# A hybrid layer on one core: DeltaNet outputs formed by channel, with the decay carried by the queries and one norm factor per token

## The chip, the cores and the metric

The kernel runs on one core of one Trainium2 chip. The time is device microseconds (us) of one execution. Each run of the program gives one time, and the median of several runs stands for the kernel. One execution was also recorded by the hardware profiler; rows of that record are called the trace.

The core has five engines that run their own instruction streams side by side: TensorE (PE in the rows; PEld is its weight load), VectorE (DVE), ScalarE (ACT), GpSimd (POOL) and SyncE (SP), which here issues nearly all DMA transfers, one after the other, in its own order. An instruction waits, with all behind it on its engine, until the tiles it reads are written and the buffers it writes are free.

## The reference

The layer takes x of 1024 tokens by 1024 channels (float32). After an RMSNorm one projection feeds two mixers. Mixer A is a gated DeltaNet of 4 heads with 128 channels each; mixer B is a dilated attention of 8 heads. Their outputs are joined and projected, added to x, and followed by a gated MLP and a last RMSNorm. The change lies in mixer A:

```python
qa = l2norm(silu(causal_dwconv(q))) * 128 ** -0.5    # also ka (without the factor) and va
gam = exp(cumsum(g))                                  # decay within a chunk
q_dec = gam * qa
attn  = dec_incl * (q k^T) * beta
# chunk after chunk, S the state (key channels by value channels):
u = u_v - w_k S
o = q_dec S + attn u                                  # tokens by channels
S = g_end * S + k_end^T u
o_a = rmsnorm(o, gdn_norm_w) * silu(z)                # per token and head, over 128 channels
```

`l2norm(x)` is x * rsqrt(sum(x^2) + eps), and `rmsnorm` is x * rsqrt(mean(x^2) + eps) * w, with eps = 1e-6.

## The kernel before

Activations lie with channels on the 128 partitions and the 1024 tokens along the free axis. A dense product of the input projection takes one column of 128 output channels: 48 matmuls of 128x512, since each fp32 product is made of three products of split halves (`xhi`, `xlo`, `whi`, `wlo`) over 8 slices of x and two halves of the tokens. There are 25 such columns, in the order of the table `DENSE` (line 42): keys, queries and values of the heads, the attention's columns, and last the four z columns, the gates.

The order of TensorE's instructions is fixed when the program is built. `Weave` (lines 49 to 120) runs generators as streams with a level each; it models TensorE's time and the time at which each tile will be ready, and always takes the ready stream of the lowest level. So the DeltaNet's chains (level 1), the preparation of keys, queries and values (3 and 4), the attention (5) and the output projection (8) are strewn among the dense matmuls (9), which fill what is left. `yield wv.need(...)` puts a stream to sleep until a tile is ready by the model, `wv.until(name)` until another stream has set a name. All matmuls carry `TOKEN` and keep this order on the chip; the order of the other engines follows from a scheduler. Buffers are rotating slots under a tag ("qa" has 4, "kT*" 4 in two parts, "kt" 4, "go" 2).

Per head of mixer A the steps are as follows. `kprep`, `qprep` and `vprep` take the convolved keys, queries and values. `qprep` (from line 641 on) transposes the queries in eight blocks of 128 tokens and sums their squares per token (`tokens`, line 568), makes the factor `rq` on VectorE and GpSimd (a power of -1/2), forms the masked products `at` of queries and keys, and stores `at` and the plain queries in DRAM (`atpark`, `qpark`). A block inverse per chunk follows, `forward_sub` with later merges, whose 32x32 blocks pass through DRAM (`xdram`, `xtdram`). When all heads are ready, `chain(h)` (line 809) goes through the 8 chunks. Each chunk makes the output twice: from the state (not for the first chunk) and from `at`, both as tokens by channels, in two halves of a PSUM bank:

```python
if c:
    mm(po[:, P:2 * P], qT, st, 0.215)
mm(po[:, :P], at, w, 0.215)
```

ScalarE scales the one by `rq`, VectorE adds the other times `gq` (`rq` times the decay), and ScalarE sums the squares of the result per token. After the last chunk, GpSimd makes `ms` to its power -1/2 and multiplies the whole output by it, and `finish(h)` transposes it back to channels by tokens (eight transposes), scales by the norm's weight `gw2` and stores it in `mixer`. When a z column is done, `dense` reloads the head's output as `og` and `gate` multiplies it with silu(z).

Of the kernel before, what the change touches and what calls it, by code (L numbers as in the profile page):

```python
# [144 lines left out]
def hybrid_layer(tc, I, out):  # L145
# [99 lines left out]
    mixer = dp.tile([8, P, S], F32, name="mixer")  # L245
    mdram = dp.tile([H, 32, 1024], F32, name="mdram")
    gdram = dp.tile([NCH * H, P], F32, name="gdram")
    xdram = dp.tile([H, 32, 1024], F32, name="xdram")
    xtdram = dp.tile([H, 32, 1024], F32, name="xtdram")
    apark = dp.tile([4, 2, P, S], F32, name="apark")  # L250
# [19 lines left out]
    def v8(t):  # L270
        return t.rearrange("p (c t) -> p c t", c=NCH)
# [69 lines left out]
    ve.memset(ones, 1.0)  # L341
    tri = tile_(sp, [P, P], F32, "tri", "r0", 1)
    sy.dma_start(tri, I["tri"])
    pick = const("pick", [P, 32])
    ve.memset(pick, 0.0)
    ve.memset(pick[:, 8:9], 1.0)
    gcw = const("gcw", [P, 12, 4], I["gcw"])
    gnw = const("gnw", [P, 1], I["gnw"])
    alog = const("alog", [P, H], bass.AP(tensor=I["a_log"].tensor, offset=I["a_log"].offset, ap=[[0, P], [1, H]]))
# [61 lines left out]
    def gates():  # L411

        yield from wv.until("rst")
        ba = sp.tile([P, NCH, 8], F32, name="ba")
        ve.tensor_tensor(ba, bat[:, :, :8], rst[:, :, None].to_broadcast([P, NCH, 8]), op=OP.mult)
        ac.activation(beta, ba[:, :, :H], AF.Exp, scale=-1.0)
        ve.tensor_scalar(beta, beta, 1.0, None, op0=OP.add)
        ve.reciprocal(beta, beta)
        zt = sp.tile([P, NCH, H], F32, name="zt")
        ve.tensor_tensor(zt, ba[:, :, H:], dtb[:, None, :].to_broadcast([P, NCH, H]), op=OP.add)  # L420
        az = sp.tile([P, NCH, H], F32, name="az")
        ac.activation(az, zt, AF.Abs)
# [12 lines left out]
        grow = tile_(sp, [NCH * H, P], F32, "grow", "osq", 1)  # L435
        ac.activation(grow, pt[:NCH * H, P:2 * P], AF.Copy)
        sy.dma_start(gdram, grow)
        ve.tensor_copy(gc, pt[:, :NCH * H].rearrange("p (c h) -> p c h", c=NCH))
# [45 lines left out]
    def gate(og, xr, anchor=None):  # L484
        y = A("zz", "ev")
        insts = [ac.activation(y, xr, AF.Tanh, scale=0.5),
                 ve.scalar_tensor_tensor(y, y, 1.0, xr, op0=OP.add, op1=OP.mult),
                 ve.tensor_tensor(og, og, y, op=OP.mult)]
        last["og"] = insts[2:]
        if anchor is not None:  # L490
            after(insts[0], anchor[0], "the softmax goes first")
            after(insts[1], anchor[1], "the softmax goes first")
# [4 lines left out]
    G = [dict() for _ in range(H)]  # L497
    T = {}
    gated = {}

    def first_keys():
        xr = [scaled(pst[2 * h:2 * h + 2], "xr", tag=("ev", "ev", "qa")[h]) for h in range(3)]
# [5 lines left out]
    def dense():  # L508
# [8 lines left out]
        for i, col in enumerate(DENSE):  # L517
# [22 lines left out]
            if kind == "k":  # L540
                T["k", h] = conv_silu(xr, 4 + h, "kT", "kT*")
                wv.add(3, kprep(h))
            elif kind == "q":
                q = conv_silu(xr, h, "qT", "qa")
                wv.add(4, qprep(h, q))
            elif kind == "v":
                v = conv_silu(xr, 8 + h, "vT", "qa")
                wv.add(4, vprep(h, v))
            elif kind == "z":
                og = gated[h] = A("og", "kT*")  # L550
                sy.dma_start(og, mixer[h])
                if i + 1 < len(DENSE):
                    put_off.append((og, xr))
                else:
                    gate(og, xr)
            else:
                if col[2] < 2:
                    sy.dma_start(apark[h, col[2]], xr)
                else:
                    t = A("avt", "ev")  # L560
                    ve.transpose(t.rearrange("p (c n j) -> p n c j", c=4, n=NCH), by_block(xr))
                    for b in range(4):
                        sq_.dma_start(avdram[h].rearrange("u x (b j) -> b u x j", b=4)[b],
                                     t[32 * b:32 * b + 32].rearrange("u (x j) -> u x j", j=32))
                wv.done.add(col)
        wv.done.add("dense")

    def tokens(src, dst, scale=None, ss=None):
# [15 lines left out]
                    ua.activation(sq, pt[:, c * P:(c + 1) * P], AF.Square, accum_out=ss[:, i:i + 1])  # L584
        return dst

    def kprep(h):
        d = G[h]
        kT = T["k", h]
# [3 lines left out]
        dec = A("dec", ("dv", "dw")[h % 2])  # L593
        gend = small("gend")
        gel = small("gel")
        rows = gdram.rearrange("(c h) t -> h c t", h=H)[h]
        sy.dma_start(v8(dec), bass.AP(tensor=rows.tensor, offset=rows.offset, ap=[[0, P]] + list(rows.ap)))
# [43 lines left out]
    def qprep(h, qT):  # L641
        d = G[h]
        yield from wv.until(("k", h))
        yield wv.need(qT, slack=SLACK)
        ssq = small("ssq")
        yield from tokens(qT, None, None, ssq)
        ve.tensor_scalar(ssq, ssq, 128.0, 128.0 * EPS, op0=OP.mult, op1=OP.add)
        rq = small("rq", 4)
        rsqrt(rq, ssq, NCH)
        at = A("at", "qa", shape=(P, NCH, P))  # L650
        for c0 in range(0, NCH, 4):
            pt = yield from next_bank("atr")
            for c in range(4):
                cs = slice((c0 + c) * P, (c0 + c + 1) * P)
                mm(pt[:, c * P:(c + 1) * P], d["kT"][:, cs], qT[:, cs], 0.215)
            for c in range(4):
                i = c0 + c
                ve.scalar_tensor_tensor(at[:, i, :], pt[:, c * P:(c + 1) * P], d["bp"][:, i:i + 1],
                                               d["dec"][:, i * P:(i + 1) * P], op0=OP.mult, op1=OP.mult)
        sy.dma_start(atpark[h], at.rearrange("p c t -> p (c t)"))  # L660
        gq = small("gq", 4)
        ve.scalar_tensor_tensor(gq, ngam[:, :, h], -1.0, rq, op0=OP.mult, op1=OP.mult)
        sy.dma_start(qpark[h], qT)
        d.update(rq=rq, gq=gq)
        wv.done.add(("q", h))

    def vprep(h, vT):
# [143 lines left out]
    def chain(h):  # L811
# [2 lines left out]
            yield from wv.until(("m", i))  # L814
            yield from wv.until(("v", i))
        d = G[h]
        kT, ktok, vtok, yt, ge, rq, gq, ke = [d[n] for n in ("kT", "ktok", "vtok", "yt", "ge", "rq", "gq", "ke")]
# [5 lines left out]
        ms = small("ms", 4)  # L823
        tg = str(h)
        st = None
        for c in range(NCH):
# [31 lines left out]
                    uv.scalar_tensor_tensor(sn, st, ge[:, c:c + 1], ps[:, 2 * P:3 * P], op0=OP.mult, op1=OP.add)  # L858
            yield wv.need(w, qa, slack=HOP)
            po = yield from next_bank("atr")  # L860
            if c:
                mm(po[:, P:2 * P], qT, st, 0.215)
            mm(po[:, :P], at, w, 0.215)

            ua.activation(vtok[:, cs], po[:, :P], AF.Copy, scale=rq[:, c:c + 1])
            if c:
                uv.scalar_tensor_tensor(vtok[:, cs], po[:, P:2 * P], gq[:, c:c + 1], vtok[:, cs], op0=OP.mult,
                                        op1=OP.add)
            if c < NCH - 1:
                st = sn  # L870
            osq = tile_(sp, [P, P], F32, "osq", "osq", 1)
            ua.activation(osq, vtok[:, cs], AF.Square, accum_out=ms[:, c:c + 1])
            wv.done.add(("c", h, c))

        uv.tensor_scalar(ms, ms, 1.0 / 128, EPS, op0=OP.mult, op1=OP.add)
        rsqrt(ms, ms, NCH)
        po_.tensor_tensor(v8(vtok), v8(vtok), ms[:, :, None].to_broadcast([P, NCH, P]), op=OP.mult)
        wv.add(1, finish(h, vtok))

    def finish(h, osb):  # L880
        for hh in range(2):
            pt = yield from next_bank("atr", osb, slack=0.8)
            for c in range(4):
                i = 4 * hh + c
                tp(pt[:, c * P:(c + 1) * P], osb[:, i * P:(i + 1) * P])
            ot = tile_(sp, [P, 512], F32, "ot", "t2", 2)
            ac.activation(ot, pt, AF.Copy, scale=gw2)
            sy.dma_start(mixer[h][:, half(hh)], ot)
        wv.done.add(("o", h))

    def by_block(t):
        return t.rearrange("p (n c u) -> p n c u", n=NCH, c=4)
# [817 lines left out]
    wv.add(9, dense())  # L1713
    for h in range(H):
        wv.add(1, chain(h))
    wv.add(5, attention())
    wv.add(8, out_proj())
    wv.add(0, mixer_splits())
# [64 lines left out]
```

## Time and profile before

| | |
|---|---|
| median of 3 runs | 1191.49 us (1191.37 to 1192.41) |
| the profiled execution | 1191.63 us |
| its span in the trace | 1189.8 us |
| granted TensorE clock | 0.998 |
| TensorE busy | 1180.1 us, 6994 matmul records |
| VectorE busy | 965.4 us |
| ScalarE busy | 573.2 us |
| GpSimd busy | 54.6 us |
| DMA moved | 156.91 MB |

The profiled execution's time holds 1.83 us outside the span. In the groups, a row names line, engine, operation, the tile written and the tiles read, the shape and the number of instructions, then the busy time in us, the mean length of one in ns, and the engine's idle time ahead of them with what ended it. In a timeline a row begins with the start and the length in us; x8 joins eight instructions that follow each other, and square brackets hold the idle time ahead. TensorE overlaps its matmuls, so the lengths of neighbours add up to more than the time that passes; starts tell what one costs. Lines 139 and 141 are those of the helpers that record every operation of the other engines, and 192 and 196 those of all matmuls and transposes, so the tiles' names tell the steps apart.

### The profile page before, as it was taken

To read this page: it belongs to the slowest core of one execution; us is meant where nothing else is said; L and a number is where in the kernel's file an instruction comes from. 1 tells how busy PE (TensorE), PEld (TensorE's weight loads), DVE (VectorE), ACT (ScalarE), POOL (GpSimd) and SP (SyncE) were. 2 spreads that over 40 slices of the span, in tenths; PEclk is the share of its full clock that TensorE was granted. 3 is DMA by queue.
4 is the path that set the end of the run, shared out by engine and by line. 5 is a ranking of instruction groups with operands and counts; after the bars stand their busy time and mean duration, and the time that the engine had idled before them with its cause. 6 is when DMAs were issued, how large, how long until landed. Compare 5 with 4: busy or idle time off the path is not lost.

```text
span 1189.8 us, 18253 instructions
## 1 busy us (share of the span) xinstructions
PE 1180.1 (99%) x6994; PEld 975.9 (82%) x6994; DVE 965.4 (81%) x1545; ACT 573.2 (48%) x1122; POOL 54.6 (5%) x49
## 2 busy tenths in 40 slices
PE   9999999999999999999999999999999999999997
PEld 7888888888777777888888888888888888888887
DVE  7776996474677787677998898989889889898987
ACT  7473444363434444555554444545444553546452
POOL 0212001013000000000000000000000000000001
PEclk9999999999999999999999999999999999999999
DMA  7423457647552414343221313122231395356734
GB/s 239 107 94 84 114 144 163 201 149 186 166 147 72 99 37 151 142 159 107 89 92 68 107 53 107 57 103 81 80 102 58 120 377 202 124 178 220 239 98 160
DMA packets 114520, 156.91 MB, mean 132 GB/s; under 512 B 54368, under 2 KB 65408, under 8 KB 114432
## 3 DMA queue, kind: packets, MB, share of 16 engines
q1 hardware_dynamic: 113712, 155.21, 41.4%
q8 instruction: 55, 0.90, 0.3%
q10 hardware_dynamic: 720, 0.53, 0.1%
q14 instruction: 33, 0.27, 0.1%
HBM read 117.68 MB, written 38.03 MB: 131 GB/s over the span
## 4 chain that ended last, share of the span: by engine, by line
PE 97%; DVE 1%; ACT 0%; issue 0%; DVEq 0%; ACTq 0%
PE ps L192 47%; PE pa L192 20%; PE dw L192 18%; PE pc L192 10%; PE ps L201 1%; PE ps L196 1%; PE warm L192 0%; DVE x1h L139 0%; ACT sm L141 0%; DVE sm L141 0%; PE pd L192 0%; DVE avt L139 0%; DVE aqkv L139 0%; DVE wke L141 0%; DVE ct L141 0%
## 5 line engine op out<-in xcount | busy, mean ns | idle before, releaser
L192 PE MATMUL dw<-pr 128*128 128x512 f32 (+1 forms) x984 | 211.4, 376 | 0.0
L192 PEld LDWEIGHTS dw<-pr 128*128 128x128 f32 x984 | 176.7, 188 | 33.7
L192 PE MATMUL ps<-xhi,whi 128*128 128x512 f32 x448 | 183.7, 410 | 0.0
L192 PE MATMUL ps<-xhi,wlo 128*128 128x512 f32 x448 | 175.2, 391 | 0.0
L192 PE MATMUL ps<-xlo,whi 128*128 128x512 f32 x448 | 174.9, 391 | 0.0
L192 PE MATMUL pa<-T,pair 128*128 128x512 f32 x528 | 126.8, 389 | 0.0
L192 PEld LDWEIGHTS pa<-T,pair 128*128 128x128 f32 x528 | 99.1, 188 | 20.6
L192 PEld LDWEIGHTS ps<-xhi,whi 128*128 128x128 f32 x448 | 84.2, 188 | 18.9 <-issue 2.7
L192 PEld LDWEIGHTS ps<-xhi,wlo 128*128 128x128 f32 x448 | 84.1, 188 | 18.3
L192 PEld LDWEIGHTS ps<-xlo,whi 128*128 128x128 f32 x448 | 84.4, 188 | 14.9 <-DVE xlo L139 0.3
L139 ACT ACTIVATE u<-pa 128x512 f32<-128x512 f32 x44 | 26.4, 599 | 114.4 <-PE pa L192 114.4
L139 DVE SCALAR_TENSOR_TENSOR y<-xu,fcw,y 128x1023 f32<-128x1023 f32 (+1 forms) x44 | 56.4, 1281 | 22.1 <-ACT y L139 22.0
L139 ACT ACTIVATE pr<-wd 128x1024 fp32r<-128x1024 f32 x33 | 35.0, 1061 | 73.4 <-DVE wd L139 35.8
L192 PE MATMUL pa<-B,A 128*128 128x512 f32 x264 | 63.5, 389 | 0.0
L192 PE MATMUL pc<-B,pair 128*128 128x512 f32 x264 | 63.4, 389 | 0.0
L192 PE MATMUL pc<-T,S 128*128 128x512 f32 x264 | 63.4, 389 | 0.0
L192 PE MATMUL pa<-T,S 128*128 128x512 f32 x264 | 63.4, 389 | 0.0
L139 DVE TENSOR_TENSOR wst<-wst 128x512 f32<-128x512 f32 x88 | 60.4, 686 | 0.8
L139 ACT ACTIVATE whi<-wst 128x1024 fp32r<-128x1024 f32 (+2 forms) x38 | 38.5, 1013 | 46.5 <-PE ps L192 38.9
L192 PE MATMUL ps<-B,pair 128*128 128x512 f32 x252 | 60.5, 389 | 0.0
L141 ACT ACTIVATE sm<-sm,mx 128x128 f32<-128x128 f32 (+7 forms) x64 | 35.5, 556 | 49.7 <-DVE mx L141 49.7
L192 PEld LDWEIGHTS pa<-T,S 128*128 128x128 f32 x264 | 49.6, 188 | 10.3
(248 smaller groups left out, 2229.8 us busy)
## 6 DMA issues: line engine op xcount, KB each, us to landing
wst<-in_wu SPq DMA_DIRECT2D x44, 512.0 KB, 3.7
wd<-in_wd SPq DMA_DIRECT2D x44, 512.0 KB, 4.4
wst<-in_wi SPq DMA_DIRECT2D x25, 512.0 KB, 4.2
upark<-y SPq DMA_DIRECT2D x22, 512.0 KB, 3.6
r<-upark SPq DMA_DIRECT2D x22, 512.0 KB, 9.9
wa<-in_wd SPq DMA_DIRECT2D x22, 256.0 KB, 3.0
apark<-aqkv SPq DMA_DIRECT2D x8, 512.0 KB, 2.7
wst<-in_wo SPq DMA_DIRECT2D x8, 512.0 KB, 3.6
```

Of the source, the lines that this page charges most:

```text
L139: return getattr(eng, op)(*a, **kw)
L141: return getattr(eng, op)(*a, **kw)
L192: tc.stamp_issue_order_token(nc.tensor.matmul(dst, lhs, rhs, start=start, stop=stop, **kw).ins, TOKEN)
L196: tc.stamp_issue_order_token(nc.tensor.transpose(dst, src, ident).ins, TOKEN)
L201: tc.stamp_issue_order_token(nc.tensor.transpose(dst, src[rows], ident[rows, rows]).ins, TOKEN)
```

## The change

Outputs of the chain are formed as channels by tokens. The matmuls' operands change places and both products add up in one PSUM region. For that the queries carry their decay: `gates` stores exp(gc) as rows in DRAM (`gamdram`), `qprep` loads a head's row to all partitions (`qd`), GpSimd multiplies it by the queries, and `qd` is stored as `qpark`. The queries are no longer transposed. Their squares, scaled by 128 x eps, are stored in `qsqpark`.

The two norms (of the query and of the output) become one factor per token, the power -1/2 of a single sum: over the 128 channels, (sum of o^2 + the scaled sum of q^2) / 128, plus a constant (`eps2`). `finish` runs once for all heads: per head it reloads the queries' squares, ScalarE squares the output, GpSimd adds both (`osq`); then 16 matmuls with a selecting matrix (`picked(h)`) sum over channels, into rows of one bank; ScalarE copies the sums out, four DMAs store them (`sdram`), one DMA reloads them as 128 rows of 32 (`ft`), GpSimd takes the power, and they are stored (`fdram`). At each z column the head's factors are loaded to all partitions (`fB`) and GpSimd multiplies `og` by them. `gate` now brings in the norm's weight `gw2`.

```diff
@@ qprep(h, qT)
-        ssq = small("ssq")
-        yield from tokens(qT, None, None, ssq)
-        ve.tensor_scalar(ssq, ssq, 128.0, 128.0 * EPS, op0=OP.mult, op1=OP.add)
-        rq = small("rq", 4)
-        rsqrt(rq, ssq, NCH)
+        qd = A("qd", "qa")
+        to_all(v8(qd), gamdram.rearrange("(c h) t -> h c t", h=H)[h])
...
         sy.dma_start(atpark[h], at.rearrange("p c t -> p (c t)"))
-        gq = small("gq", 4)
-        ve.scalar_tensor_tensor(gq, ngam[:, :, h], -1.0, rq, op0=OP.mult, op1=OP.mult)
-        sy.dma_start(qpark[h], qT)
-        d.update(rq=rq, gq=gq)
+        po_.tensor_tensor(qd, qd, qT, op=OP.mult)
+        sy.dma_start(qpark[h], qd)
+        ac.activation(qT, qT, AF.Square, scale=128.0 * EPS ** 0.5)
+        sy.dma_start(qsqpark[h], qT)
@@ chain(h)
+            po = po[:, :P]
             if c:
-                mm(po[:, P:2 * P], qT, st, 0.215)
-            mm(po[:, :P], at, w, 0.215)
-
-            ua.activation(vtok[:, cs], po[:, :P], AF.Copy, scale=rq[:, c:c + 1])
-            if c:
-                uv.scalar_tensor_tensor(vtok[:, cs], po[:, P:2 * P], gq[:, c:c + 1], vtok[:, cs], op0=OP.mult,
-                                        op1=OP.add)
+                mm(po, st, qT, 0.215, True, False)
+            mm(po, w, at, 0.215, c == 0, True)
+            ua.activation(vtok[:, cs], po, AF.Copy)
             if c < NCH - 1:
                 st = sn
-            osq = tile_(sp, [P, P], F32, "osq", "osq", 1)
-            ua.activation(osq, vtok[:, cs], AF.Square, accum_out=ms[:, c:c + 1])
             wv.done.add(("c", h, c))
-
-        uv.tensor_scalar(ms, ms, 1.0 / 128, EPS, op0=OP.mult, op1=OP.add)
-        rsqrt(ms, ms, NCH)
-        po_.tensor_tensor(v8(vtok), v8(vtok), ms[:, :, None].to_broadcast([P, NCH, P]), op=OP.mult)
-        wv.add(1, finish(h, vtok))
+        sy.dma_start(mixer[h], vtok)
+        wv.done.add(("e", h))
@@ finish: once for all heads (before: per head, 8 transposes, 2 scaled copies, 2 stores)
+    def finish():
+        for h in range(H):
+            yield from wv.until(("e", h))
+            osq, qsq = A("osq", "kT*"), A("qsq", "kt")
+            osqs.append(osq)
+            sy.dma_start(qsq, qsqpark[h])
+            ac.activation(osq, G[h]["vtok"], AF.Square)
+            po_.tensor_tensor(osq, osq, qsq, op=OP.add)
+        for h in range(H):
+            wv.done.add(("o", h))
+        pt = yield from next_bank("atr", *osqs, slack=1.0)
+        for h in range(H):
+            for g in range(4):
+                o = 32 * g
+                mm(pt[o:o + 32, :256], picked(h), by_quarter(osqs[h])[:, g], 0.107, h == 0, h == H - 1,
+                   tile_position=(0, o))
+        sums = tile_(sp, [P, 256], F32, "sums", "t2", 2)
+        ac.activation(sums, pt[:, :256], AF.Identity, scale=1.0 / 128, bias=eps2)
+        for g in range(4):
+            sq_.dma_start(sdram.rearrange("h (c g i) -> g h c i", g=4, i=32)[g],
+                          sums[32 * g:32 * g + H].rearrange("h (c i) -> h c i", i=32))
+        ft = tile_(sp, [P, 32], F32, "ft", "osq", 1)
+        flat = "h (a t) -> (h a) t"
+        sq_.dma_start(ft, sdram.rearrange(flat, t=32))
+        f4 = ft.rearrange("p (a t) -> p a t", t=NCH)
+        po_.tensor_tensor(f4, f4, mhalf[:, None, :].to_broadcast([P, 4, NCH]), op=OP.pow)
+        sq_.dma_start(fdram.rearrange(flat, t=32), ft)
+        wv.done.add("f")
@@ dense(), z columns, and gate()
+                yield from wv.until("f")
                 og = gated[h] = A("og", "kT*")
                 sy.dma_start(og, mixer[h])
+                if not fB:
+                    fB.append(A("fB", "go"))
+                to_all(fB[0], fdram[h])
+                po_.tensor_tensor(og, og, fB[0], op=OP.mult)
...
-                 ve.tensor_tensor(og, og, y, op=OP.mult)]
+                 ve.scalar_tensor_tensor(og, og, gw2, y, op0=OP.mult, op1=OP.mult)]
```

`to_all(dst, rows)` is a DMA that reads the same rows for each of the 128 partitions.

On TensorE, at the end of a head's chain, before (vtok is the head's output, xhi, xlo, whi and wlo the dense matmuls, ct the state, qat the loaded queries and `at`):

```order
L192 MATMUL ps<-r,um 128x128
L192 MATMUL ps<-ct,kT 128x128
L196 MATMUL ps<-ident,vtok 128x128 x4
L192 MATMUL ps<-xhi,whi 128x512
L192 MATMUL ps<-xlo,whi 128x512
L192 MATMUL ps<-xhi,wlo 128x512
L192 MATMUL ps<-wke,ktok 128x128
L192 MATMUL ps<-ct,qat 128x128
L192 MATMUL ps<-w,qat 128x128
```

And after, at the same place:

```order
L192 MATMUL ps<-wke,ktok 128x128
L192 MATMUL ps<-qat,ct 128x128
L192 MATMUL ps<-qat,w 128x128
L192 MATMUL ps<-xhi,whi 128x512
L192 MATMUL ps<-xlo,whi 128x512
L192 MATMUL ps<-xhi,wlo 128x512
L192 MATMUL ps<-ct,kT 128x128
```

The four transposes of vtok are gone, and the two output matmuls of a chunk stand where they stood, with their operands changed.

On GpSimd, from the queries to the block inverse, a piece of the difference (rq is the power for the queries, xi and x the buffers of the inverse, nk the keys' factor):

```order
 L139 TENSOR_TENSOR nk<-ssk,phalf 128x8 x4
+L139 TENSOR_TENSOR qd<-qd,qT 128x1024
 L139 MEMSET xi 128x1024
 L139 AFFINE_SELECT xi<-xi 128x1024
-L139 TENSOR_TENSOR rq<-ssq,mhalf 128x8 x3
-L139 MEMSET x_1709 128x1024
-L139 MEMSET x_1723 128x1024
-L139 TENSOR_TENSOR rq<-ssq,mhalf 128x8
-L139 COPY mark<-x_1723 1x1
+L139 TENSOR_TENSOR qd<-qd,qT 128x1024 x2
+L139 MEMSET x_1663 128x1024
+L139 MEMSET x_1677 128x1024
```

Two multiplications by the decay come between the inverse's first steps and its later ones, in the place of the powers. Further on, before the attention's gates, GpSimd's order after is this (pb is a tile of the attention's probabilities):

```order
L139 TENSOR_TENSOR osq<-osq,qsq 128x1024
L139 TENSOR_TENSOR ft<-ft,mhalf 128x32
L139 TENSOR_TENSOR og<-og,fB 128x1024
L139 MEMSET pb 128x512
L139 TENSOR_TENSOR og<-og,fB 128x1024 x3
L139 MEMSET pb 64x256
L139 MEMSET pb 128x512 x2
```

The multiplications by the factor stand between the memsets of the attention.

On SP, after the norm factor's sums, after the change (avt and in_wi are the attention's values and the next weights):

```order
L139 DMA og<-mixer 128x1024
L139 DMA sdram<-sums 32x1x32 x4
L139 DMA ft<-sdram 128x32
L139 DMA fdram<-ft 128x32
L139 DMA fB<-fdram 128x1024
L139 DMA mixer<-oT 128x512
L139 DMA fB<-fdram 128x1024
L139 DMA wst<-in_wi 128x1024
```

The factor's way through DRAM stands ahead of a weight load, and SP issues nothing else until each step's data are there.

More of the change, by code (lines that the diff above doesn't have):

```diff
@@ L247, in hybrid_layer @@
     gdram = dp.tile([NCH * H, P], F32, name="gdram")
+    gamdram = dp.tile([NCH * H, P], F32, name="gamdram")
+    qsqpark = dp.tile([H, P, S], F32, name="qsqpark")
+    sdram = dp.tile([H, S], F32, name="sdram")
+    fdram = dp.tile([H, S], F32, name="fdram")
     xdram = dp.tile([H, 32, 1024], F32, name="xdram")
@@ L343, in hybrid_layer, with picked @@
     sy.dma_start(tri, I["tri"])
-    pick = const("pick", [P, 32])
-    ve.memset(pick, 0.0)
-    ve.memset(pick[:, 8:9], 1.0)
+    picks = const("picks", [P, 64])
+    ve.memset(picks, 0.0)
+    ve.memset(picks[:, 32:33], 1.0)
+    eps2 = const("eps2", [P, 1])
+    ve.memset(eps2, 128.0 * EPS * EPS)
+    def picked(j):
+        return picks[:, 32 - j:64 - j]
+    pick = picked(8)
     gcw = const("gcw", [P, 12, 4], I["gcw"])
@@ L437, in gates @@
         sy.dma_start(gdram, grow)
+        gamrow = tile_(sp, [NCH * H, P], F32, "gamrow", "w0", 1)
+        ac.activation(gamrow, grow, AF.Exp)
+        sy.dma_start(gamdram, gamrow)
         ve.tensor_copy(gc, pt[:, :NCH * H].rearrange("p (c h) -> p c h", c=NCH))
@@ L499, in hybrid_layer @@
     gated = {}
+    fB = []
     def first_keys():
@@ L585, in tokens, with to_all @@
         return dst
+    def to_all(dst, rows):
+        sy.dma_start(dst, bass.AP(tensor=rows.tensor, offset=rows.offset, ap=[[0, P]] + list(rows.ap)))
     def kprep(h):
@@ L595, in kprep @@
         gel = small("gel")
-        rows = gdram.rearrange("(c h) t -> h c t", h=H)[h]
-        sy.dma_start(v8(dec), bass.AP(tensor=rows.tensor, offset=rows.offset, ap=[[0, P]] + list(rows.ap)))
+        to_all(v8(dec), gdram.rearrange("(c h) t -> h c t", h=H)[h])
         po_.affine_select(v8(dec), v8(dec), pattern=[[0, NCH], [1, P]], compare_op=OP.is_ge, fill=NEG,
@@ L816, in chain @@
         d = G[h]
-        kT, ktok, vtok, yt, ge, rq, gq, ke = [d[n] for n in ("kT", "ktok", "vtok", "yt", "ge", "rq", "gq", "ke")]
+        kT, ktok, vtok, yt, ge, ke = [d[n] for n in ("kT", "ktok", "vtok", "yt", "ge", "ke")]
         if not ct:
@@ L822, in chain @@
         ps = bank(("asc", "ch")[h // 2])
-        ms = small("ms", 4)
         tg = str(h)
@@ L878, in chain @@
-        wv.add(1, finish(h, vtok))
[L880 to L889, printed above, removed]
+        sy.dma_start(mixer[h], vtok)
@@ new lines, in chain @@
+        wv.done.add(("e", h))
+    osqs = []
+    def finish():
[26 more added lines that the diff above has]
+        wv.done.add("f")
@@ L1715, in hybrid_layer @@
         wv.add(1, chain(h))
+    wv.add(1, finish())
     wv.add(5, attention())
```

## The prediction

> **What bounds the kernel now.** I read the page's busy times and the chain of waits first, then the windows of the stretch that the change touches (about 100 to 350 us), then its transposes in the groups and in TensorE's own timeline.
>
> ```profile
> span 1189.8 us, 18253 instructions
> PE 1180.1 (99%) x6994; PEld 975.9 (82%) x6994; DVE 965.4 (81%) x1545; ACT 573.2 (48%) x1122; POOL 54.6 (5%) x49
> PE 97%; DVE 1%; ACT 0%; issue 0%; DVEq 0%; ACTq 0%
> 100.00:150.00 50.00, 50.00 (x255) 42.42 (x254) 43.06 (x90) 20.50 (x53) 4.50 (x2) 1.00 0.45 119
> 150.00:200.00 50.00, 50.00 (x364) 42.22 (x363) 40.01 (x75) 21.39 (x62) 7.16 (x4) 1.00 0.58 150
> 200.00:250.00 50.00, 49.41 (x557) 43.83 (x556) 29.55 (x71) 22.49 (x78) 0.35 (x2) 1.00 0.64 189
> 250.00:300.00 50.00, 49.53 (x313) 44.05 (x312) 27.73 (x71) 24.12 (x83) 15.96 (x12) 1.00 0.60 163
> 300.00:350.00 50.00, 49.96 (x521) 37.64 (x521) 34.44 (x103) 19.37 (x60) 1.43 (x3) 1.00 0.57 163
> ```
>
> The columns of a window are its length, then busy time and instruction count of TensorE, its weight loads, VectorE, ScalarE and GpSimd, then the granted clock, the DMA share and GB/s. TensorE (PE) is busy for 1180.1 of 1189.8 us and carries 97% of the chain. In the five windows it stands idle for 0, 0, 0.59, 0.47 and 0.04 us. So work taken off VectorE or ScalarE shortens nothing by itself; only two things count: TensorE's own instructions, removed or added, and new waits of TensorE. The clock is 1.00 throughout, so the clock gives and takes nothing.
>
> **The change part by part.** *Transposes removed.* Per head, eight transposes of the queries and eight of the chain's output go, 64 in all.
>
> ```profile
> L196 PE MATMUL ps<-ident,qT 128*128 128x128 f32 x32 | 4.1, 272 | 0.0
> L196 PE MATMUL ps<-ident,vtok 128*128 128x128 f32 x32 | 4.5, 272 | 0.0
> 109.40 0.39 PE L192 MATMUL ps<-xlo,whi 128*128 128x512 f32 x1
> 109.62 0.39 PE L192 MATMUL ps<-xhi,wlo 128*128 128x512 f32 x1
> 109.86 1.03 PE L196 MATMUL ps<-ident,qT 128*128 128x128 f32 x8
> 110.65 0.48 PE L192 MATMUL ps<-xhi,whi 128*128 128x512 f32 x1
> 110.96 0.40 PE L192 MATMUL ps<-xlo,whi 128*128 128x512 f32 x1
> ```
>
> The mean of 272 ns is the length of one that overlaps its neighbours, so I price by starts. A dense matmul starts every 0.225 us (109.40 to 109.62; 0.228 over longer stretches). From 109.62 to 110.96 there are two dense matmuls and eight transposes: 1.34 - 2 x 0.228 = 0.886, or 0.111 each with the switches to and from them. 64 x 0.111 = 7.1 us off. [...]
>
> *Chain.* Each chunk still has its two output matmuls; only their operands change places and they now accumulate, so nothing there. ScalarE loses 32 squares of the output and half of the 64 token squares, VectorE 28 additions of 0.346 us: load off engines that TensorE hardly waits for.
>
> *Added: 16 narrow matmuls* of 256 columns for the joint sums.
>
> ```profile
> 20.29 0.39 PE L192 MATMUL ps<-xhi,wlo 128*128 128x512 f32 x1
> 20.60 3.66 PE L192 MATMUL ps<-xt,wba 128*32 128x256 f32 x64
> 24.20 0.50 PE L192 MATMUL ps<-xhi,whi 128*128 128x512 f32 x1
> ```
>
> These are the same form: 256 columns, 32 results. The program issues 32 there (eight slices of x by four column groups; the trace shows each as two records, hence x64), and from start to start they take 3.60 us, so 0.1125 each. 16 x 0.1125 = 1.8, and a block's switches to and from the dense matmuls, about 0.2 (24.20 to 24.53 is 0.33 where 0.23 is usual, and as much at the other edge), make 2.0. Without switches it is 1.8; if all four heads came as blocks of their own, each with switches, 2.5 is the upper end. Sum on TensorE: -7.1 + 2.0 = -5.1.
>
> *Moved under VectorE: GpSimd's new multiplications.* GpSimd (POOL) goes from 4 multiplications of 128x1024 to 12: four of decay by query, four sums of squares, four factors by gated output. One costs 1.9 us there, and the next rows show what it does to VectorE.
>
> ```profile
> L139 POOL TENSOR_TENSOR vtok<-vtok,ms 128x1024 f32<-128x1024 f32 x4 | 7.6, 1898 | 0.3
> 44.56 1.27 DVE L139 SCALAR_TENSOR_TENSOR kT<-xr,gcw,kT 128x1023 f32<-128x1023 f32 x1
> 46.35 6.81 DVE L139 SCALAR_TENSOR_TENSOR kT<-xr,gcw,kT 128x1023 f32<-128x1023 f32 x4
> 48.16 5.95 POOL L139 TENSOR_SCALAR_AFFINE_SELECT dec<-dec 128x1024 f32<-128x1024 f32 x3 [1.32 <-DMA dec<-gdram]
> 293.58 1.75 DVE L139 TENSOR_TENSOR wlo<-wst,whi 128x1024 fp32r<-128x1024 f32 x1
> ```
>
> A VectorE step alone takes 1.27 us; four of the same beside GpSimd work take 6.81, so 1.70 each, and a subtraction runs to 1.75. [...]
>
> Where does that reach TensorE? First, the block inverse (about 172 to 200 us), where the solved blocks pass through DRAM to the merges:
>
> ```profile
> 172.57 0.69 DVE L139 TENSOR_TENSOR xr<-ps,rstdB 128x512 f32<-128x512 f32 x1 [0.30 <-PE ps L192]
> 177.19 1.12 DVE L139 COPY mt<-xi 128x1024 f32<-128x1024 f32 x1
> 178.49 0.37 SPq L139 DMA_DIRECT2D xdram<-xi  x1
> 192.81 1.99 SPq L139 DMA_DIRECT2D x<-xdram  x4
> x<-xdram SPq DMA_DIRECT2D x8, 64.0 KB, 2.4
> 196.25 2.21 PE L192 MATMUL ps<-x,um 32*32 32x32 f32 x128
> ```
>
> The last x load is issued at about 194.8 and lands 2.4 later, at 197.2, while the merges start at 196.25 and their second half needs it about 1.1 later: no slack. Afterwards TensorE's order has 360 dense matmuls ahead of the merges instead of 333 (27 x 0.228 = +6.2 us) and 32 transposes fewer (-3.6), so the second half is due near 200.0. The copy at 177.19 now stands behind one more scaling (0.69), fed by products that TensorE reaches about 2.5 us later than the copy's last input now, and possibly behind two of the decay multiplications (up to 2 x 1.9 = 3.8). So x is there between 199.7 and 203.5, and the wait is 0 to 3.5 us. I take 0.8, near the lower end: the multiplications come singly, so at most a part of each meets one of VectorE's long steps.
>
> *The chain's first load.* For each head SP now issues a broadcast load of the decays and a store of the squares more, 512 KB each (the store of the queries was there before), and the last head's come between the inverse and the chain, with all the stores of the values ahead of this load.
>
> ```profile
> 208.04 0.32 SPq L139 DMA_DIRECT2D vtok<-vdram  x1
> 223.57 1.05 PE L192 MATMUL ps<-vtok,um 128*128 128x128 f32 x8
> 200.00:215.00 15.00, 15.00 (x295) 12.85 (x294) 7.86 (x10) 4.70 (x14) 0.35 (x2) 1.00 0.89 232
> ```
>
> vtok of the last head has 15 us from issue to use, and the use moves to about 226.5, with the merges (+2.7). In SP's new order I put the issue between 208 and 216 and the landing 4 to 7 us behind it, at 212 to 223, DMA being 0.89 busy already; 2 to 3 us of scaling follow, so vtok is ready between 214 and 226. So 0 to 1 us if the landing slips further, taken at 0.
>
> *The tail of the chain and the gates.* Before, SP stored two halves of each head's output; now it has one store per head, then a round trip of 4 sums, 1 reload, 1 power of 128x32 on GpSimd, 1 store, then one broadcast load and one multiplication per head. GpSimd's power is priced from its narrow ones:
>
> ```profile
> L139 POOL TENSOR_TENSOR rq<-ssq,mhalf 128x8 f32<-128x8 f32 x4 | 9.8, 2439 | 66.3 <-DVE ssq L139 66.3
> L139 POOL TENSOR_TENSOR ms<-ms,mhalf 128x8 f32<-128x8 f32 x4 | 6.5, 1636 | 12.3 <-DVE ms L141 12.2
> 311.70 0.38 SPq L139 DMA_DIRECT2D wst<-in_wi  x1
> 326.39 0.69 SPq L139 DMA_DIRECT2D wst<-in_wi  x1
> 324.58 0.53 POOL L139 MEMSET pb<- 128x512 f32 x1 [30.32 <-PE ps L192]
> 355.45 1.26 ACT L141 ACTIVATE pb<-ps 32x128 f32<-32x128 f32 x4 [2.68 <-DVE pt L141]
> ```
>
> 1.64 us for 8 columns makes 32 columns at most 6.6 (an estimate, four times as much). With six transfers in a row, each some 2 to 4 us from issue to landing, the round trip holds SP about 20 us (estimate) from 301 on. Behind it stands a weight load that was issued at 326.39 and whose column has two others ahead of it, each 48 dense matmuls (11 us), so its use is near 358: no cost. The factor is first used at a z gate, past 400: none either. On GpSimd the first multiplication by the factor waits for its load, and behind it stands the memset of the tile for the attention's next transposed probabilities (pb), made at 324.58 and first filled by ScalarE at 355.45; the attention comes some 10 us earlier in TensorE's new order, so the memset is due by 345. With the factor landing by 328 it ends at 331: 14 us of room, no cost. But the four multiplications by the factor come free as soon as it is there and fall beside the softmax of the attention (315 to 343), whose VectorE steps TensorE waits for at once when they are late. Between 0 and 4 x 1.9 = 7.6; the window 300 to 350 had 0.04 us of idle, since dense matmuls fill, so 0.5.
>
> *Possibly gained:* two waits of the chain on work that becomes less.
>
> ```profile
> 242.03 0.49 PE L192 MATMUL ps<-ct,kT 128*128 128x128 f32 x2 [0.45 <-DVE ct L141]
> 256.24 0.49 PE L192 MATMUL ps<-wke,ktok 128*128 128x128 f32 x2 [0.47 <-ACT w L141]
> ```
>
> Together 0.9 of the 1.06 idle in those two windows; not counted, but kept as an end.
>
> Sum: -7.1 + 2.0 + 0.8 + 0.5 = -3.8. The profiled execution took 1191.63, 0.14 above the median of 1191.49; so 1187.8 profiled, 1187.7 as median.
>
> **The rivals.** (B) No new wait, and the chain's bubbles gone: -5.1 - 0.9 = -6.0, 1185.5. For it: VectorE's 28 additions and ScalarE's squares leave the chain; against: merges without slack. (C) Waits eat the gain: the merges 2.5 (of 0 to 3.5), softmax 1.5: -7.1 + 2.0 + 4.0 = -1.1, 1190.4. For it: VectorE at 40 of 50 us in the window of the merges. (D) Slower: each multiplication by the factor holds VectorE's softmax up and TensorE waits for all of it: 7.6 + 0.8 - 5.1 = +3.3, 1194.8. It decides once more than 4.3 us of the 7.6 land, a little over two of the four. Against it: the idle time of 0.04 us in 300 to 350, where dense matmuls stand ready to fill. (E) The transposes are worth the 272 ns of their own rows: 64 x 0.272 = 17.4 - 2.0 = 15.4 off, 1176. The starts above speak against it. [...]
>
> **How the numbers follow.** A forecast 0.47 (1187.7; own range 1186.4 to 1189.0: both waits at nothing, or 1.3 us more of them), B 0.17, C 0.19, D 0.15, E 0.02. 0.2% is 2.4 us, about what a measurement here can tell from no change. Faster by more: A, B, E = 0.66; within: C, 0.19; slower: D, 0.15. The range reaches from B with 0.2 less for the added matmuls and 0.4 more for the transposes (the group of vtok is busy 0.4 us longer than that of qT), 1184.9, to C with the full us for the chain's first load, 1191.4. It leaves out D and E, 0.17.
>
> **What would show it.** Right: TensorE's busy time about 5 us less, no transposes of qT or vtok, idle near 11; the merges near 199 with a wait of about 1 us. Wrong: idle ahead of the softmax's matmuls at 310 to 345 with VectorE as the releaser (D or C); idle ahead of the first matmul on vtok (then the extra stores cost); or the group of 16 narrow matmuls taking more than 2.5 us.

## The result and the profile after

The changed kernel takes 1189.9 us (median of 22 runs, 1187.86 to 1194.19), the kernel before 1192.05 us beside it (22 runs, 1191.37 to 1193.23). The ratio is 0.9985 with a 95% interval of 0.9979 to 0.999: 1.2 to 2.5 us faster, a little over half of the forecast 3.8. The profiled execution took 1188.58 us, 3.05 less than that of before, so it lies near the lower end of its own runs; it holds 2.08 us outside its span of 1186.5. How widely they spread is a second finding: the runs of before lie within 1.9 us, those of after within 6.3.

The page of after, span and busy times, and then the windows of the same stretch (the columns are as in the prediction):

```profile
span 1186.5 us, 18081 instructions
PE 1175.1 (99%) x6962; PEld 971.1 (82%) x6962; DVE 960.6 (81%) x1506; ACT 554.6 (47%) x996; POOL 65.9 (6%) x50
```

```profile
100.00:150.00 50.00, 50.00 (x247) 42.29 (x246) 44.88 (x83) 18.34 (x23) 6.93 (x4) 1.00 0.53 156
150.00:200.00 50.00, 50.00 (x270) 41.84 (x269) 44.60 (x75) 18.34 (x30) 7.18 (x4) 1.00 0.62 164
200.00:250.00 50.00, 49.51 (x645) 43.72 (x639) 24.92 (x55) 16.91 (x49) 0.36 (x2) 1.00 0.63 203
250.00:300.00 50.00, 48.21 (x302) 42.41 (x302) 24.26 (x66) 19.28 (x53) 11.37 (x8) 1.00 0.71 216
300.00:350.00 50.00, 49.04 (x543) 36.53 (x542) 34.53 (x104) 18.72 (x60) 13.08 (x5) 1.00 0.58 174
```

TensorE's busy time fell by 5.0 us (1180.1 to 1175.1), but its idle time in the last two windows grew from 0.51 to 2.75 us. TensorE's waits, of after first and then of before, name the tiles (what waits and for whom; us in total, how often, the longest). A row of after need not be the same step as that of before:

```profile
PE ps L192 <- ACT w L141: 1.8, 1, 1.8
PE ps L201 <- DVE sm L141: 0.9, 2, 0.5
PE ps L192 <- DVE ct L141: 0.2, 1, 0.2
```

```profile
PE ps L192 <- ACT w L141: 0.5, 1, 0.5
PE ps L192 <- DVE ct L141: 0.4, 1, 0.4
PE ps L201 <- DVE sm L141: 0.3, 1, 0.3
```

The chain waits 1.8 us for one w, and the softmax 0.9 us for sm. In the timeline of VectorE around the longer wait, and of TensorE behind it, the reason can be read:

```profile
269.23 1.14 DVE L139 TENSOR_TENSOR aqkv<-ps,rstdB 128x512 f32<-128x512 f32 x1 [0.35 <-PE ps L192]
270.45 1.23 DVE L139 STREAM_TRANSPOSE avt<-aqkv 128x1024 f32<-128x1024 f32 x1
271.61 1.39 DVE L139 TENSOR_TENSOR wlo<-wst,whi 128x1024 fp32r<-128x1024 f32 x1
272.92 0.34 DVE L141 TENSOR_SCALAR wke<-ps,ke 128x128 f32<-128x128 f32 x1
270.64 0.39 PE L192 MATMUL ps<-r,um 128*128 128x128 f32 x2
273.62 0.49 PE L192 MATMUL ps<-wke,ktok 128*128 128x128 f32 x2 [1.79 <-ACT w L141]
```

The matmul on r that starts at 270.64 gives the input of a chain step on VectorE (wke, 272.92); ScalarE's w, which the row names, itself sat idle for 1.15 us until wke. That step stands behind the transposition of the attention's values and the subtraction that makes a weight's low half (wlo), a 2.5 us block that nothing in the chain needs. In TensorE's order the next matmuls of the chain follow at once, with no dense ones between, so TensorE stands.

It is the 26th of the chain's 28 products with wke. In the kernel before, the 26th had four transposes of the output and three dense matmuls ahead of it and waited for nothing; the same block on VectorE came later, with a wke between its two steps (the subtraction followed at 281.41). TensorE, then VectorE, before:

```profile
269.31 0.60 PE L196 MATMUL ps<-ident,vtok 128*128 128x128 f32 x4
270.45 0.38 PE L192 MATMUL ps<-wke,ktok 128*128 128x128 f32 x2
280.01 1.25 DVE L139 STREAM_TRANSPOSE avt<-aqkv 128x1024 f32<-128x1024 f32 x1
281.18 0.31 DVE L141 TENSOR_SCALAR wke<-ps,ke 128x128 f32<-128x128 f32 x1
```

So both orders changed at this step, and the transposes that the change took away were part of the work that had stood ahead of it.

### The profile page after: what moved, and what is told of

The parts are those of the page before. It is cut to its first block, busy times and chain, and to the rows that moved or that the text cites. A ratio compares the mean times of both kernels' runs of the same rounds, so it can differ in the third digit from the quotient of the medians.

```text
span 1186.5 us, 18081 instructions
## 1 busy us (share of the span) xinstructions
PE 1175.1 (99%) x6962; PEld 971.1 (82%) x6962; DVE 960.6 (81%) x1506; ACT 554.6 (47%) x996; POOL 65.9 (6%) x50
## 4 chain that ended last, share of the span: by engine, by line
PE 97%; DVE 1%; ACT 0%; issue 0%; DVEq 0%; ACTq 0%
PE ps L192 47%; PE pa L192 20%; PE dw L192 18%; PE pc L192 10%; PE ps L201 1%; PE ps L196 1%; PE warm L192 0%; DVE x1h L139 0%; ACT sm L141 0%; DVE sm L141 0%; PE pd L192 0%; DVE wlo L139 0%; DVE aqkv L139 0%; DVE avt L139 0%; DVE wke L141 0%
## 5 line engine op out<-in xcount | busy, mean ns | idle before, releaser
L139 DVE TENSOR_TENSOR wlo<-wst,whi 128x1024 fp32r<-128x1024 f32 (+2 forms) x38 | 45.8, 1206 | 17.8 <-ACT whi L139 17.8
L192 PEld LDWEIGHTS pc<-T,S 128*128 128x128 f32 x264 | 49.6, 188 | 10.3
```

Source lines behind the costliest of these rows:

```text
L139: return getattr(eng, op)(*a, **kw)
L192: tc.stamp_issue_order_token(nc.tensor.matmul(dst, lhs, rhs, start=start, stop=stop, **kw).ins, TOKEN)
```

## The experiments

The runs, with the median of the kernel before on the same chip; each run's trace is one execution of it.

| run | median us (lowest to highest, runs) | before, same chip |
|---|---|---|
| e1, unaltered | 1189.23 (1188.03 to 1192.51, 6) | 1192.49 |
| e2, no squares | 1191.28 (1189.51 to 1195.55, 12) | 1192.49 |
| e3, queries transposed | 1203.02 (1201.27 to 1203.68, 4) | 1192.49 |
| e4, no multiplication by the factor | 1189.3 (1188.21 to 1191.04, 8) | 1192.49 |
| e5, chain first | 1187.77 (1186.9 to 1188.8, 5) | 1192.31 |
| e6, chain and softmax first | 1187.19 (1186.97 to 1188.09, 5) | 1192.31 |
| e7, 64 more transposes | 1198.15 (1196.43 to 1199.24, 4) | 1192.31 |
| e8, unaltered | 1188.89 (1187.88 to 1191.07, 9) | 1192.31 |
| e9, unaltered | 1189.82 (1 run) | 1192.0 (1 run) |
| e10, unaltered | 1187.86 (1 run) | 1192.0 (1 run) |

**Is the loss fixed or does it come and go? (e1, e8, unaltered)**

> The changed kernel once more, unaltered, for a second trace and the spread of its runs. Theory 1 (TensorE's own work fell by 5 us, and fixed waits in the chain and the softmax, 1.8 and 0.9 us, give part of it back): this trace shows the same two waits with the same lengths, and the time is 1188 to 1190. Theory 2 (the waits come from transfers that land late, and so differ from one execution to the next): the waits stand elsewhere or have other lengths, above all at the merges of the block inverse, and executions differ by 2 us and more.

> The changed kernel unaltered, beside the runs of the same chip: 1188 to 1190, with some executions of 1191 and more. Should the traced execution be one of the longer ones, its trace shows a stretch of half clock in the middle of the program, behind a wait of over 1.5 us; if the longer ones have another cause, the clock stays at 1.00 and a longer wait shows.

Both traces show the two waits at the same places, with 1.8 and 0.9 us in e1 and 1.6 and 0.9 us in e8, and spans of 1186.6 and 1186.9. No wait at the merges or at the first load of the chain appears. So the fixed part of theory 1 holds; but executions do differ by 3 to 4.5 us, which it doesn't explain. Neither trace caught a long execution.

**Contention, by leaving out the squares (e2)**

```diff
-        ac.activation(qT, qT, AF.Square, scale=128.0 * EPS ** 0.5)
-        sy.dma_start(qsqpark[h], qT)
...
-            sy.dma_start(qsq, qsqpark[h])
             ac.activation(osq, G[h]["vtok"], AF.Square)
-            po_.tensor_tensor(osq, osq, qsq, op=OP.add)
```

> Leaves out the queries' squares from the norm factor: no square on ScalarE, no store and reload (8 transfers of 512 KB less), no addition on GpSimd. If the extra traffic beside the merges and the chain's first load, or the GpSimd additions beside the chain, cost the missing 2 us (contention), this is 1.5 to 2.5 us faster than the changed kernel and its runs spread less. If the waits come from the order of VectorE's instructions, it is within 0.7 us of the changed kernel.

It became slower by 2.0 us than the unaltered kernel on that chip, which neither case of the expectation gave. TensorE's waits in its trace (an execution of 1194.12 us), then VectorE's and GpSimd's rows at the longest of them:

```profile
PE ps L201 <- DVE sm L141: 3.8, 3, 2.6
PE ps L192 <- ACT w L141: 1.6, 1, 1.6
317.04 3.26 DVE L141 TENSOR_SCALAR sm<-sm,mx 128x384 f32<-128x384 f32 x2
316.95 2.35 POOL L139 TENSOR_TENSOR og<-og,fB 128x1024 f32<-128x1024 f32 x1 [5.58 <-DMA fB<-fdram]
```

With the traffic and GpSimd's additions gone, the chain's wait is still 1.6 us. Contention is not the main cause of the chain's wait; VectorE's order remains. The orders were planned anew, so the time is no measure of the traffic alone. In this plan a multiplication by the factor falls beside a softmax's division: two steps that took 0.72 us in the profile of after (at 322.98) took 3.26, TensorE waited 2.6 us for them, and the granted clock was 0.50 from 321.6 to 325.0. That is what rival D had named: VectorE's softmax held up beside a multiplication by the factor, and TensorE waiting for it, here 2.6 us.

**The price of a transpose, first try (e3)**

```diff
+        ssq = small("ssq")
+        yield from tokens(qT, None, None, ssq)
         qd = A("qd", "qa")
```

> The changed kernel with the 32 transposes of the queries and ScalarE's 32 squares per token put back, their sums unused. [...]

It is 13.8 us slower than the unaltered kernel, where 32 transposes at the 0.111 us of the prediction make 3.6. One new wait holds over half of the 13.8, at the chain's first load (SP's own rows, then TensorE's):

```profile
215.41 0.60 SPq L139 DMA_DIRECT2D qpark<-qd  x1
221.23 1.02 SPq L139 DMA_DIRECT2D vtok<-vdram  x1
231.94 1.65 PE L192 MATMUL ps<-vtok,um 128*128 128x128 f32 x6 [7.73 <-ACT um L139]
```

In this plan vtok's load stands behind the last head's stores of queries, squares and `at`, is issued at 221.23 (215.33 in the unaltered kernel), and TensorE waits 7.73 us; the granted clock is 0.50 from 227.9 to 238.1. So the time of this run says nothing on the price, but it shows how near the first load is to the path. Its trace does bear on the price: where eight transposes of the queries stand between dense matmuls, 110.60 to 111.94, the starts give 1.34 - 2 x 0.228 = 0.884, or 0.11 each, as before.

**The multiplications beside the softmax (e4)**

```diff
                 to_all(fB[0], fdram[h])
-                po_.tensor_tensor(og, og, fB[0], op=OP.mult)
```

> Leaves out GpSimd's four multiplications of the gated output by the factor (the loads of the factor stay), so the output lacks the norm. If they hold VectorE up beside the softmax, the waits on sm (0.9 us) go and it is 0.5 to 1 us faster; if the softmax waits for a VectorE step that stands ahead of it in the order, no change beyond 0.3 us and the waits on sm remain.

The time is that of the unaltered kernel (1189.3 against 1189.23), and a wait on sm of 0.5 us remains, with a new one of 0.9 on VectorE's scaling (aqkv) elsewhere, behind a VectorE step (vT, at 191.42) that took 3.18 us beside GpSimd's multiplication by the decay. On the median these four multiplications cost nothing that can be measured. The traced execution is a long one, 1190.53 us, and its clock stays at 1.00 up to the last norm.

**Only VectorE's order (e5, e6)**

```diff
-            if i + 1 < len(DENSE):
-                nxt = wk(None, raw.pop())
+            later = i in (15, 19)          # e5: i == 15 alone
+            if not later:
+                nxt = following()          # makes whi and wlo of the next column, loads the one after
...
                     yield 0.0
+                    if later and (hh, k) == (0, 4 if i == 15 else 0):
+                        nxt = following()
+                        after(lows_made[-1], last["wke" if i == 15 else "div"], "the chain and the softmax go first")
```

> The changed kernel with TensorE's order unaltered, and on VectorE one weight subtraction (wlo) placed behind three steps of the chain instead of ahead of them. Theory 1 (the 1.8 us wait of the chain comes from VectorE's order: a chain step stands behind the attention's scaling, its transposition and this subtraction): the wait falls to 0.3 to 0.7 us and the time by 1 to 1.5 us. If half-speed stretches of TensorE's clock follow that wait in some executions, the spread of the runs shrinks too and the median falls by 1.5 to 3 us. Theory 2 (GpSimd's additions hold VectorE): the wait stays over 1.2 us.

> As the run before, and a second weight subtraction placed behind the last steps of one softmax. Theory 1: the two waits on sm (0.9 us together) shrink to under 0.3, and the time is 1.5 to 2.3 us below the changed kernel's profiled 1188.6, near 1186.7; with both waits gone the runs keep within 2 us of each other, as those of the kernel before do. If the spread has another cause, it stays at 4 us and more.

TensorE's order is word for word that of the changed kernel, and on VectorE nothing between 115 and 960 us is moved but these subtractions; SP exchanges a few neighbouring transfers. e5 is 1.1 us faster than e8 on the same chip and e6 1.7 us (1187.19 against 1188.89); against before, e6's ratio is 0.9959, interval 0.9947 to 0.9972, e5's 0.9963 (0.995 to 0.9975). So e6 has the lowest median of all, 5.1 us under the kernel before it, though the 0.6 us to e5 lie within the ranges of the two. TensorE's waits in e6, and VectorE's rows at the place of the chain:

```profile
PE ps L201 <- DVE sm L141: 0.8, 3, 0.4
PE ps L192 <- ACT w L141: 0.5, 1, 0.5
```

```profile
271.02 1.24 DVE L139 STREAM_TRANSPOSE avt<-aqkv 128x1024 f32<-128x1024 f32 x1
272.18 0.32 DVE L141 TENSOR_SCALAR wke<-ps,ke 128x128 f32<-128x128 f32 x1
```

The chain's wait fell from 1.8 to 0.5 us: VectorE's order made 1.3 of it. The waits on sm hardly shrank in sum (0.9 to 0.8); that half of the expectation failed. The wait of 0.53 us that the second move was aimed at is gone, one of 0.38 stayed, and two of 0.2 came up near 334, behind a division that took 2.98 us, beside a multiplication by the factor, where it took 0.78 in the profile of after. The spread of the runs is now 1.1 us instead of 3.2 in e8, with five runs against nine, eight of which lie within 1.9: that the spread shrank is not shown.

**64 idle transposes (e7)**

```diff
         wv.done.add("f")
+        for b in range(16):
+            if b % 4 == 0:
+                pd = yield from next_bank("atr")
+            for i in range(4):
+                tp(pd[:, i * P:(i + 1) * P], osqs[b % 4][:, i * P:(i + 1) * P])
```

> The changed kernel with 64 idle transposes of 128x128 in one block behind the 16 narrow matmuls. [...] If transposes do not count as work for the clock, the granted clock falls to 0.5 in or behind the block and the matmuls after it take about twice their time for some 3 us; otherwise it stays at 1.00.

The block in TensorE's timeline, then the windows over it and behind it:

```profile
303.11 1.93 PE L192 MATMUL ps<-osq,picks 128*32 128x256 f32 x32
304.98 7.21 PE L196 MATMUL ps<-ident,osq 128*128 128x128 f32 x64
311.94 0.47 PE L192 MATMUL ps<-xhi,whi 128*128 128x512 f32 x1
```

```profile
305.00:312.00 7.00, 7.00 (x69) 7.00 (x65) 0.00 (x0) 0.47 (x1) 0.00 (x0) 1.00 0.78 246
312.00:316.00 4.00, 4.00 (x29) 3.03 (x27) 1.15 (x4) 0.00 (x0) 1.95 (x1) 1.00 0.59 158
```

From 304.98 to 311.94 are 6.96 us, or 0.109 each (7.1 us at the 0.111 of the prediction), and the clock stays at 1.00 in and behind the block. The time rose by 9.3 us over e8, 2.3 more than the block; the same trace shows where some of it went, at the chain's wait, 30 us ahead of the block (timeline, then a window):

```profile
271.57 2.04 DVE L139 TENSOR_TENSOR wlo<-wst,whi 128x1024 fp32r<-128x1024 f32 x1
274.23 0.49 PE L192 MATMUL ps<-wke,ktok 128*128 128x128 f32 x2 [2.42 <-ACT w L141]
276.49 0.63 PE L192 MATMUL ps<-xhi,wlo 128*128 128x512 f32 x1
276.92 0.63 PE L192 MATMUL ps<-xhi,whi 128*128 128x512 f32 x1
```

```profile
275.30:278.70 3.40, 3.40 (x12) 2.83 (x12) 0.70 (x2) 0.18 (x1) 0.00 (x0) 0.50 1.17 211
```

Here the subtraction ran 2.04 us, beside one of GpSimd's additions (2.37 us from 270.16), instead of 1.39 in the profile of after, the wait grew to 2.42, and right behind it the granted clock was 0.50 for 3.4 us: dense matmuls start 0.43 apart (276.49 to 276.92) instead of 0.23. At these starts the stretch holds half the work, so it costs an estimated 1.7 us (half of the 3.4) on top of the wait. Two further waits in this trace are new, 1.5 us on pb and 0.9 us on xr.

**Two more executions of the unaltered kernel (e9, e10)**

> The changed kernel unaltered, one traced execution. If it is one of the longer ones (over 1190.5), half clock for 3.4 us stands right behind the wait of the chain near 273, and VectorE's subtraction ahead of it is longer than 1.4 us because it meets GpSimd's addition; if not, the wait is 1.6 to 1.8 and the clock stays at 1.00.

> The same as the look before, another execution: over 1190.5 with a stretch of half clock behind the wait near 273, or under it with the clock at 1.00 up to the last norm.

e9 took 1189.82 us and e10 1187.86, one run each. Both have the chain's wait of 1.6 us at full clock. But e9 differs behind the softmax (VectorE, TensorE, then windows of e9):

```profile
338.49 1.92 DVE L139 TENSOR_TENSOR wlo<-wst,whi 128x1024 fp32r<-128x1024 f32 x1
341.20 0.47 PE L201 MATMUL ps<-ident,sm 64*128 64x64 f32 x4 [1.23 <-DVE sm L141]
```

```profile
340.00:343.00 3.00, 1.45 (x14) 1.08 (x15) 2.86 (x10) 0.60 (x2) 0.00 (x0) 1.00 0.95 170
343.00:346.50 3.50, 3.50 (x11) 2.29 (x11) 1.18 (x5) 0.00 (x0) 1.70 (x1) 0.51 0.46 167
```

The same VectorE row and the multiplication by the factor next to it, in e10 and in e9:

```profile
338.36 1.22 DVE L139 TENSOR_TENSOR wlo<-wst,whi 128x1024 fp32r<-128x1024 f32 x1
334.00 2.40 POOL L139 TENSOR_TENSOR og<-og,fB 128x1024 f32<-128x1024 f32 x1 [4.12 <-DMA fB<-fdram]
```

```profile
336.95 2.38 POOL L139 TENSOR_TENSOR og<-og,fB 128x1024 f32<-128x1024 f32 x1 [4.47 <-DMA fB<-fdram]
```

In e10 the multiplication ends at 336.4, before the subtraction; in e9 the factor came 3 us later, it ran until 339.33, and the subtraction that began at 338.49 lasted 1.92 instead of 1.22 us. The wait on sm grew from 0.5 to 1.23, and half clock followed for 3.4 us. The expectation had named this, a subtraction that meets a GpSimd step and half clock behind the wait, but at the other one of the two waits, and with the wrong bound: e9 is under 1190.5. So one part of the spread is shown: between e10 and e9 a GpSimd multiplication moved beside a VectorE step, the step took 0.70 us longer and the wait 0.7 us, and the 3.4 us at half clock behind it, in which dense matmuls start 0.43 apart (343.17 to 343.59), cost TensorE an estimated further 1.7 us. Other parts lie elsewhere: e4's long execution has no half clock on its way, and at the start the fourth dense matmul begins at 6.85 us in the profiled execution and at 6.01 in e10. The two longest of the 22 runs (1194.00 and 1194.19) have a mean granted clock of 0.995, against 0.998 in the profiled one and 0.996 in e9. This fits more half clock in them, but it is not shown; no execution of the unaltered kernel over 1191 was traced.

## Why the prediction was right, and where it was off

The sign and the range held (1184.9 to 1191.4), and so did the way: TensorE's own work fell. The size, as a median, did not: 2.15 us instead of 3.8. That is outside the forecast's own range (1186.4 to 1189.0) and nearer the rival C by time (1190.4), though not by its place; it is also less than the 2.4 us that the prediction took for no change, a case that it gave 0.19.

- *TensorE's work:* -5.1 forecast, -5.0 in busy time. The transposes measured 0.109 each in e7's block against 0.111; the 16 narrow matmuls took 1.87 us from start to start, against 2.0:

```profile
300.89 1.93 PE L192 MATMUL ps<-osq,picks 128*32 128x256 f32 x32
302.76 0.50 PE L192 MATMUL ps<-xhi,whi 128*128 128x512 f32 x1
```

  Rival E is out: one record lasts 272 ns in the rows of before, but in a row the transposes start 0.109 us apart.
- *The merges:* +0.8 forecast, nothing measured. The collision was there, but hidden: the last x load was issued by 196.5, the merges began at 199.44 with no wait. GpSimd's decay multiplication took 2.88 us and the VectorE step beside it 2.49, where its like took 1.27 at 189.79, but it fell behind the copy that the merges need and not ahead of it:

```profile
181.38 1.14 DVE L139 COPY mt<-xi 128x1024 f32<-128x1024 f32 x1
189.79 1.27 DVE L139 SCALAR_TENSOR_TENSOR vT<-xr,gcw,vT 128x1022 f32<-128x1022 f32 x1
190.45 2.88 POOL L139 TENSOR_TENSOR qd<-qd,qT 128x1024 f32<-128x1024 f32 x1 [3.82 <-DMA qd<-gamdram]
191.92 2.49 DVE L139 SCALAR_TENSOR_TENSOR vT<-xr,gcw,vT 128x1021 f32<-128x1021 f32 x1
199.44 2.21 PE L192 MATMUL ps<-x,um 32*32 32x32 f32 x128
```

  In the traces of e4 and e5 the same collision took more, 3.18 and 3.37 us for the VectorE step, and TensorE waited 0.9 and 0.7 us behind it, for a scaling (aqkv) and not at the merges. That a collision costs VectorE up to the 1.9 us of one GpSimd instruction, as the ends of 3.8 and 7.6 take it, with the 0.8 and the 0.5 of the sum chosen below them, was the author's estimate: no run shows such a limit. In its place the runs showed steps longer by 1.22 us beside the 2.88 here, by 1.91 and 2.10 in e4 and e5, and by 2.54 for two steps beside 2.35 in e2.

- *The chain's first load:* taken at 0, and 0 in all five traces of the changed kernel as it is; its fragility is shown by e3.
- *The chain's waits:* here the working failed. The prediction put the chain at nothing, as it takes "load off engines that TensorE hardly waits for", and kept two waits as a possible gain of 0.9. These two did shrink, from 0.47 to nothing (the 20th product with wke, now at 258.22) and from 0.45 to 0.21. But at the 26th a wait of 1.79 us opened, for which it had no term: VectorE's new order has a block of foreign work ahead of that step, and TensorE's has nothing to do meanwhile. VectorE's load fell, from 965.4 to 960.6 us busy, and that did not prevent a wait that comes from what stands ahead in its queue. e5 shows that 1.3 of the 1.8 come from the place of one subtraction; the 0.5 that stay are not taken apart.
- *The softmax:* +0.5 forecast, +0.6 measured (0.3 to 0.9) in the profiled execution, but for another reason than the multiplications: a weight subtraction that stands between the steps (339.42), with no dense matmuls ahead of TensorE's next ones. Before, it stood there too (342.00), with three dense matmuls ahead of them. The prediction had named idle time here with VectorE as the releaser as a sign for D or C; the sign came, at a tenth of D's price. A softmax step held up beside a multiplication by the factor, as D has it, was seen in some executions only: 0.7 us in e9, a wait of 2.6 us in e2's plan.
- *The sum:* -5.0 + 1.3 - 0.2 + 0.6 = -3.3, as between the spans (by tile, as in the rows of waits: 1.3 is 1.8 less the 0.5 that went). That this is near the forecast of -3.8 is in part luck: the 0.8 for the merges, which cost nothing, stood in for the chain's 1.1. The step from the profiled pair (3.05) to the medians (2.15) is what the prediction had no term for: "the clock gives and takes nothing" held for before and for the profiled execution of after, and not for e9. A wait on TensorE was priced at its length, when in e7 and e9 the half clock behind one cost an estimated 1.7 us more. How much of that step is half clock is not shown: two runs near the median (1189.32 and 1189.81) have the clock of the profiled one, 0.998. In e9 the half clock came although TensorE was busy for 1.45 of the 3 us ahead of it.

## What to carry to other kernels

When TensorE is the bound, price the instructions taken away by their starts, and then read the queue of the engine that feeds each tight hand-over, step by step: a 2.5 us block of foreign work in front of one chain step made a wait of 1.8 us out of the 5 gained, and moving a part of that block returned 1.1 with TensorE's order untouched. Ask also what stood behind the instructions that go. Some waits of TensorE cost more here than their length, by 3.4 us of half clock behind waits of 1.23 us (e9) and 2.42 us (e7); take a wide spread of times as a sign to look for such waits, and do not judge by one profiled execution.

## What the runs showed of the hardware

- Half clock came in single stretches of 3.4 us behind waits of 1.23 us (e9), 2.42 us (e7) and 2.6 us (e2) and for 10.2 us around one of 7.73 us (e3), but not behind the waits of 1.6 to 1.8 us in the five traces of the unaltered kernel. So the length of a wait alone does not decide it; what does stays open.
- Two steps of a softmax's division took 3.26 us beside a GpSimd multiplication of 2.35 us (e2), against 0.72 in the profile of after (322.98).
- GpSimd's four multiplications by the factor, each of two 128x1024 tiles, took 2.39 us on average, against 1.90 for the one before the change, whose second input was eight numbers per partition, repeated. The groups of after:

```profile
L139 POOL TENSOR_TENSOR og<-og,fB 128x1024 f32<-128x1024 f32 x4 | 9.6, 2390 | 19.8 <-DMA fB<-fdram 14.0 <-issue 5.8
L139 POOL TENSOR_TENSOR ft<-ft,mhalf 128x32 f32<-128x32 f32 x1 | 5.4, 5439 | 25.1 <-DMA ft<-sdram 25.1
```

- Its power of 128x32 took 5.44 us, below the estimated 6.6.
